# Attention probabilities in a hybrid decoder layer: transposes on fp32r operands fed by SBUF-to-SBUF transfers, and splits moved to the head of a unit

## The chip, the cores and the metric

The kernel runs on one core of a Trainium2 chip. The core has five engines that run side by side and are kept in step by semaphores: TensorE (matmuls and transposes), VectorE, ScalarE, GpSimd and SyncE. In the profile they are called PE, DVE, ACT, POOL and SP; PEld is TensorE's load of the stationary operand. Sixteen DMA engines move data between memories; a transfer is issued by one of the engines' queues (here SP's, and for a few transfers ACT's). The on-chip memory SBUF holds the operands, PSUM receives what TensorE produces.

The metric is the device time of one execution in microseconds. Before the change three runs took 390.55, 390.63 and 391.24 us, median 390.63.

## The reference

One layer of a causal decoder for 256 tokens of width 1024, all in float32. From a normalised input one wide projection gives queries, keys and values of two attention branches and the logits of two merge gates.

```
h = rmsnorm(x, g_mix);  proj = h @ w_in
o_a = nsa_attention(...)        # 8 heads, 2 key groups; compressed, selected and window branches, gated
o_b = dilated_attention(...)    # 12 heads in 3 groups, mixed by their softmax denominators
mixed = sigmoid(g_A) * (o_a @ w_proj_nsa) + sigmoid(g_B) * (o_b @ w_proj_dil)
x = x + mixed @ w_out
x = x + conv_ffn(rmsnorm(x, g_ffn))
return rmsnorm(x, g_final)
```

Each attention branch is softmax(q k - slope * distance) @ v under a causal mask. The product with v contracts over the keys, so the probabilities, which come out of the softmax with queries on the partitions and keys along the free axis, have to be transposed once.

## The kernel before

**Arithmetic.** Most products are made of three fp32r matmuls: each operand is split into a high part (rounded to fp32r) and a low part (the remainder, also fp32r), and high x high, high x low and low x high are summed in PSUM. fp32r is a four-byte type that TensorE takes in one pass; an engine that writes a tile of this type rounds. `split_hi` (line 127, ScalarE) and `split_lo` (line 131, VectorE, for a few units GpSimd) do this for the weights. Smaller products, among them probabilities times v, are plain fp32, which TensorE takes as two instructions each. A transpose is one TensorE instruction with the data as stationary operand and an identity as moving operand.

**Units.** The work is a list of units, mostly one block of 128 x 2048 weights (1 MB) each: 0 to 15 project queries, keys and values, 16 to 19 the logits of gate A, 20 to 23 those of gate B (`ev_ml`), 24 to 26 the projections of the two branches with the merge, 27 to 30 w_out, and the rest the ffn. The schedule is written out by hand in one loop over the units (lines 1127 to 1222). In each turn the host code emits, for every engine in this order, the load of the unit five ahead (SP), then some work of the attention, then the low part of the next unit's weights (`lo_of(i + 1)`), then the unit's matmuls, the high part for the unit after next (`hi_of(i + 2)`) and the evacuation of the unit's result, and then the attention's TensorE work. Each engine executes its own instructions in the order of emission. Loads wait for one of three raw weight buffers to come free, which the low part of an earlier unit does.

**Attention items.** Twelve items lie on units 9 to 20, one each: six of the NSA branch (class `Nsa`), six of the dilated one (class `Dil`), each with one or two heads and one half (t) of the queries; unit 11 also has the compressed branch (`Cmp`). An item at unit i goes through these steps:

- unit i: `split` (dilated items with t = 1 only) at the head, and `qk` after the matmuls: TensorE makes the scores in PSUM.
- unit i + 1: `sm` (VectorE adds the distances and takes the minimum, ScalarE the exponential, into a tile E, two buffers), and behind the weights' low part `sm2` (VectorE multiplies E by the gates and the inverse sums).
- unit i + 2: `tr`, behind the unit's matmuls: TensorE transposes E in blocks of 128 x 128 into PSUM (lines 881, 993 and 808); 8 blocks for an NSA item, 6 for a dilated one, 2 for the compressed branch.
- unit i + 3: `te` at the head: ScalarE, and for a part VectorE, copies the transposed blocks to SBUF (lines 886, 887, 998, 999, 813).
- units 14, 17, 20 and 23: `pv` for three items at a time (lines 894 and 1018), and in the unit after it `fin`, the split of the result.

**The split of a dilated item** (lines 935 to 939) copies one half of q and k as high parts to the other partitions (three ScalarE copies into a tile DK) and takes the low parts (two VectorE subtractions). `dil_tiles`, at unit 15, makes the tiles and zeroes a part of them on GpSimd. In the loop both stand behind `te` and `sm`:

```
for it in at(i - 3):  it.te()
for it in at(i - 1):  it.sm()
if i == FIRST_ITEM + 6:  dil_tiles()
for it in at(i):  if isinstance(it, Dil): it.split()
```

**Places in SBUF.** A tile's tag names its place. Tag MA (8 KB per partition) holds a part of the first weights and then gate A's logits; tag MB (8 KB) a part of the first weights, then the tile XC for the compression MLP until unit 8, and from unit 20 gate B's logits. Between units 8 and 20 MB is idle.

Of the kernel before, what the change touches and what calls it, by code (L numbers as in the profile page):

```python
# [11 lines left out]
F32 = mybir.dt.float32  # L12
# [6 lines left out]
S = 256  # L19
# [73 lines left out]
def build(ctx, tc, a, out):  # L93
# [143 lines left out]
    def bc(R, n):  # L237
# [16 lines left out]
    first = [att.tile([128, n * 768 + 8 * (t == "QS")], F32, name="first", tag=t)  # L254
             for n, t in zip(CHUNKS, ("QS", "MA", "qb", "MB", "kb", "vb"))]
    M = {}
# [56 lines left out]
    def ev_cmp(u):  # L313
        R = rt["R"]
        t = att.tile([128, 2, 2, 128], F32, name="E", tag="E", bufs=2)
        f = att.tile([128, 4, 256], F32, name="XC", tag="MB")
        p = u.p.rearrange("p i (s two) -> p two i s", two=2)
# [144 lines left out]
    ML = {}  # L462

    def ev_ml(i):
        def f(u):
            ab = i // 4
            if i % 4 == 0:
                ML[ab] = att.tile([128, 8, S], F32, name="ML%d" % ab, tag="MA" if ab == 0 else "MB")
            ev_k(ML[ab], 2 * (i % 4))(u)
        return f  # L470
# [7 lines left out]
    def mix_out(i, h, hook=None):  # L478

        if h == 0:  # L480
            mixh.append(att.tile([128, 4, S], F32R, name="mixh", tag="E", bufs=2))
            mixl.append(att.tile([128, 4, S], F32R, name="mixl", tag="PT", bufs=3))
        hs = slice(4 * i + 2 * h, 4 * i + 2 * h + 2)
        ho = slice(2 * h, 2 * h + 2)
        m = ML[0][:, hs]
        V.tensor_tensor(out=m, in0=m, in1=ML[1][:, hs], op=OP.add)
        A.activation(mixh[i][:, ho], m, AF.Copy)
        if hook:
            hook()
        V.tensor_sub(mixl[i][:, ho], m, mixh[i].bitcast(F32)[:, ho])  # L490

    def mm_pd(u):
        for h in range(4):
            p = mmT(u, [2 * h, 2 * h + 1], 2, OB['h'], OB['l'], "do"[h % 2])
            mB = ML[1][:, 2 * h:2 * h + 2]
            V.tensor_tensor(out=mB, in0=p, in1=mB, op=OP.mult)
            if h % 2:
                mix_out(0, h // 2)

    def mm_pn(i):  # L500
        def f(u):
            for h in range(2):
                p = mmT(u, [2 * h, 2 * h + 1], 4, oah, oal)
                m = ML[0][:, 4 * i + 2 * h:4 * i + 2 * h + 2]
                V.tensor_tensor(out=m, in0=p, in1=m, op=OP.mult)
                if i:
                    mix_out(1, h, None if h else between)
        return f
# [256 lines left out]

    class Cmp:
        def by_keys(self):
            p = cmp_["cm"][:, 256:512]
# [36 lines left out]
        def tr(self):  # L805
            p = pd([S], "o")
            for t in range(2):
                T.transpose(p[:, t * 128:(t + 1) * 128], self.E[:, t].rearrange("p h c -> p (h c)"), ident)
            self.pt = p

# [13 lines left out]

    class Nsa:

# [16 lines left out]
        def sm(self):  # L843
            js, t, nk, n = self.js, self.t, self.nk, self.n
            E = att.tile([128, 1024], F32, name="E", tag="E", bufs=2)
            self.E = E[:, :n * nk].rearrange("p (a k) -> p a k", a=n)
            st_ = att.tile([128, 24], F32, name="ast", tag="ast", bufs=2)
# [26 lines left out]
        def tr(self):  # L874
            self.sl = [(c, k, b, g) for c in range(len(self.js)) for k in range(self.nk // 128)
                       for b in range(2) for g in range(2)]
            self.pt = []
            for q in range(2):
                p = pd([4, 128], "t")
                for i, (c, k, b, g) in enumerate(self.sl[4 * q:4 * q + 4]):  # L880
                    T.transpose(p[:, i], self.E[:, 4 * c + 2 * g + b, k * 128:(k + 1) * 128], ident)  # L881
                self.pt.append(p)

# [38 lines left out]

    class Dil:

# [43 lines left out]
        def sm(self):  # L968
            ss, t, nk = self.ss, self.t, self.nk
            E = att.tile([128, 1024], F32, name="E", tag="E", bufs=2)  # L970
            self.E = E[:, :3 * len(ss) * nk].rearrange("p (c g k) -> p c g k", c=len(ss), g=3)
            st_ = att.tile([128, 24], F32, name="ast", tag="ast", bufs=2)
# [14 lines left out]
        def tr(self):  # L987
            self.sl = [(c, k, q) for k in range(self.nk // 128) for q in range(3) for c in range(len(self.ss))]
            self.pt = []
            for i in range(0, 6, 4):  # L990
                p = pd([4, 128], "t")
                for n, (c, k, q) in enumerate(self.sl[i:i + 4]):
                    T.transpose(p[:, n], self.E[:, c, q, k * 128:(k + 1) * 128], ident)
                self.pt.append(p)

# [84 lines left out]
    k = 0  # L1080
# [35 lines left out]
    def at(i):  # L1116
        return items.get(i, [])
# [9 lines left out]
    for i, u in enumerate(units):  # L1127
        load_to(i + LA)
        if i == 9:
            cmp_sum()  # L1130
        for it in batches.get(i - 1, []):
            it.fin()
        for it in at(i - 3):
            it.te()
        if i == 11:
            cmp_kv_ev()
        for it in at(i - 1):
            it.sm()
        if i == FIRST_ITEM + 6:
            dil_tiles()  # L1140
        for it in at(i):
            if isinstance(it, Dil):
                it.split()
        if i > 2 and i != 6:
# [17 lines left out]
        if i in (23, 24):  # L1162
            m = ML[i - 23]
            A.activation(m, m, AF.Sigmoid)
        if i == NFIRST:
# [121 lines left out]
```

## Time and profile before

| what | value |
|---|---|
| median of three runs | 390.63 us |
| the profiled execution | 391.16 us |
| its span | 389.3 us |
| TensorE granted clock, mean | 0.997 |
| TensorE, VectorE, ScalarE, GpSimd busy | 382.1, 300.0, 216.9, 31.3 us |
| moved by DMA | 72.62 MB, mean 187 GB/s |
| transposes of NSA, dilated, compressed items | 48, 36, 2 |
| units 9 to 23 on TensorE (start to end) | 47.4 to 164.1 us |

The span is the time between the first and the last recorded instruction; what is left of the execution's time lies outside it. Busy time of TensorE is counted from modelled ends of pipelined instructions, and overlapping instructions count once, so its share says little about how densely it works; the distance between the starts of successive instructions says more. Unit boundaries are found in the chain of waits by the groups of 32 and 16 matmuls of a unit (lines 186 and 191). A time in the chain's rows is the start in the span, followed by the length; in rows of one line's instructions the three durations are the minimum, median and maximum in nanoseconds.

### The profile page before, as it was taken

What the parts mean: (1) busy time and instruction counts of PE and PEld (TensorE: products, weight loads), DVE (VectorE), ACT (ScalarE), POOL (GpSimd) and SP (SyncE); (2) the same over time, 40 slices, a digit from 0 to 9 for tenths busy, and PEclk for the clock granted to TensorE, in tenths of its full rate; (3) what the DMA queues carried; (4) which work ended last, traced back from release to release, by engine and by line L of the source; (5) the groups of instructions that cost most, each with busy time, mean ns of one, the idle gap of its engine ahead of it and who ended that gap; (6) DMA issues with size and microseconds to landing.
All of it is one profiled execution on the core that took longest, in us unless ns stands there. A gap on an engine that the chain in (4) does not pass through costs nothing.

```text
span 389.3 us, 8064 instructions
## 1 busy us (share of the span) xinstructions
PE 382.1 (98%) x3420; PEld 375.7 (97%) x3420; DVE 300.0 (77%) x510; ACT 216.9 (56%) x306; POOL 31.3 (8%) x60
## 2 busy tenths in 40 slices
PE   8999999999999999999999999999999999999993
PEld 7999999999999999999999999999999999999993
DVE  6797599994877776558887789778696886968764
ACT  6876536775974665754634666626365363643613
POOL 8100000001000000250333000000000000000001
PEclk9999999999999999999999999999999999999998
DMA  8999253445234345452547266574644646446202
GB/s 292 404 354 382 110 215 119 166 148 221 108 109 128 132 159 184 159 184 111 189 170 280 104 223 216 204 231 178 241 173 153 229 168 253 162 163 224 103 0 109
DMA packets 11844, 72.62 MB, mean 187 GB/s; under 512 B 1312, under 2 KB 1696, under 8 KB 4128
## 3 DMA queue, kind: packets, MB, share of 16 engines
q1 hardware_dynamic: 11376, 71.25, 50.1%
q10 hardware_dynamic: 432, 0.85, 0.6%
q8 instruction: 27, 0.44, 0.5%
q14 instruction: 9, 0.07, 0.0%
HBM read 71.05 MB, written 1.05 MB: 185 GB/s over the span
## 4 chain that ended last, share of the span: by engine, by line
PE 94%; DVE 2%; ACT 2%; issue 0%; POOL 0%; POOLq 0%; ACTq 0%
PE ps_d L186 26%; PE ps_d L191 13%; PE ps_o L186 13%; PE ps_s L617 8%; PE ps_t L617 7%; PE ps_o L191 6%; PE ps_d L343 3%; PE ps_d L290 3%; PE ps_t L186 2%; PE ps_o L894 1%; PE ps_o L533 1%; PE ps_t L881 1%; PE ps_s L186 1%; PE ps_o L1018 1%; PE ps_t L191 1%; PE ps_t L1064 1%
## 5 line engine op out<-in xcount | busy, mean ns | idle before, releaser
L131 DVE TENSOR_TENSOR wlo<-raw,whi 128x2048 fp32r<-128x2048 f32 (+2 forms) x62 | 134.6, 2176 | 2.8 <-ACT whi L127 2.4
L127 ACT ACTIVATE whi<-raw 128x2048 fp32r<-128x2048 f32 (+2 forms) x62 | 115.1, 1858 | 32.7 <-DMA raw<-in_wts_dram 28.8
L186 PE MATMUL ps_d<-hTh,whi 128*128 128x256 f32 x384 | 90.4, 281 | 0.0
L186 PE MATMUL ps_d<-hTl,whi 128*128 128x256 f32 x384 | 89.3, 278 | 0.0
L186 PEld LDWEIGHTS ps_d<-hTh,whi 128*128 128x128 f32 x384 | 72.3, 188 | 0.9 <-issue 0.7
L186 PEld LDWEIGHTS ps_d<-hTl,whi 128*128 128x128 f32 x384 | 72.3, 188 | 0.0
L191 PE MATMUL ps_d<-hTh,wlo 128*128 128x256 f32 x384 | 47.9, 277 | 0.0
L191 PEld LDWEIGHTS ps_d<-hTh,wlo 128*128 128x128 f32 x384 | 45.8, 188 | 0.0
L186 PE MATMUL ps_o<-hTh,whi 128*128 128x256 f32 x160 | 36.9, 277 | 0.0
L186 PE MATMUL ps_o<-hTl,whi 128*128 128x256 f32 x160 | 36.8, 276 | 0.0
L572 ACT ACTIVATE C<-U,small 128x256 f32<-128x256 f32 x22 | 12.0, 594 | 43.7 <-DVE U L568 43.7
L186 PEld LDWEIGHTS ps_o<-hTl,whi 128*128 128x128 f32 x160 | 30.0, 188 | 0.0
L186 PEld LDWEIGHTS ps_o<-hTh,whi 128*128 128x128 f32 x160 | 30.0, 188 | 0.0
L576 DVE SCALAR_TENSOR_TENSOR C<-U,small,C 128x256 f32<-128x256 f32 x44 | 19.4, 482 | 7.5 <-ACT C L572 7.4
L858 ACT ACTIVATE E<-E,ast 128x256 f32<-128x256 f32 (+1 forms) x32 | 14.2, 451 | 10.1 <-DVE ast L853 10.1
L191 PE MATMUL ps_o<-hTh,wlo 128*128 128x256 f32 x160 | 19.8, 276 | 0.0
L191 PEld LDWEIGHTS ps_o<-hTh,wlo 128*128 128x128 f32 x160 | 18.9, 188 | 0.0
L568 DVE TENSOR_TENSOR U<-ps_d,R 128x512 f32<-128x512 f32 x6 | 4.1, 690 | 13.7 <-PE ps_d L191 10.7
L1123 DVE STREAM_TRANSPOSE X<-xT 32x256 f32<-32x256 f32 x32 | 13.9, 436 | 0.4
L1243 POOL TENSOR_TENSOR tiny<-cst,tiny 128x1 f32<-128x1 f32 x2 | 0.4, 192 | 166.7 <-ACT sq L1242 166.7
L131 POOL TENSOR_TENSOR wlo<-raw,whi 128x1024 fp32r<-128x1024 f32 x3 | 7.7, 2571 | 74.0 <-ACT whi L127 74.0
L617 PE MATMUL ps_s<-whi,al 128*128 128x256 f32 x88 | 12.1, 276 | 0.0
(272 smaller groups left out, 743.1 us busy)
## 6 DMA issues: line engine op xcount, KB each, us to landing
raw<-in_wts_dram SPq DMA_DIRECT2D x59, 1024.0 KB, 4.8
first<-in_first_dram SPq DMA_DIRECT2D x7, 384.0 KB, 6.0
raw<-in_wts_dram SPq DMA_DIRECT2D x2, 560.0 KB, 9.5
xn<-in_xn_dram SPq DMA_DIRECT2D x2, 512.0 KB, 9.5
w1k<-in_wts_dram SPq DMA_DIRECT2D x2, 512.0 KB, 7.0
w1v<-in_wts_dram SPq DMA_DIRECT2D x2, 512.0 KB, 7.9
xT<-in_xT_dram SPq DMA_DIRECT2D x1, 1024.0 KB, 7.0
gf<-in_g_final_dram ACTq DMA_DIRECT2D x1, 512.0 KB, 3.6
```

Of the source, the lines that this page charges most:

```text
L127: A.activation(u.hi[:, u.o + c0:u.o + c1], u.raw[:, c0:c1], AF.Copy)
L131: (eng or V).tensor_sub(u.lo[:, u.o + c0:u.o + c1], u.raw[:, c0:c1], u.hi.bitcast(F32)[:, u.o + c0:u.o + c1])
L186: T.matmul(po, l, r, start=start and bank not in banks, stop=False, skip_group_check=True)
L191: T.matmul(po, l, r, start=False, stop=stop and n == len(ks) - 1, skip_group_check=True)
L290: T.matmul(u.p[:, i], l[:, kt, i * 128:i * 128 + 128], r[:, kt], start=kt == 0 and i == 0 and q == 0, stop=kt == 7 and q == 2, skip_group_ ...
L343: T.matmul(u.p[:, i], l[:, kt, i * 128:i * 128 + 128], r[:, kt], start=kt == 0 and i == 0 and q == 0, stop=kt == 7 and q == 2, skip_group_ ...
L568: V.tensor_tensor(out=U[:, :, 2:], in0=u.p, in1=bc(rt["R2"], 2), op=OP.mult)
L572: A.activation(C[:, c], U[:, c, 2:], AF.Identity, scale=CW(2, t), bias=CB[:, t:t + 1])
L576: V.scalar_tensor_tensor(C[:, c], U[:, c, w:w + S], CW(w, t), C[:, c], op0=OP.mult, op1=OP.add)
L617: T.matmul(ffn["y"][t][ch][:, b:e] if own is None else own, x[:, kt, t * 128:t * 128 + 128], w[:, kt, ch * 512 + b:ch * 512 + e], start=st ...
L858: A.activation(self.E[:, i], self.E[:, i], AF.Exp, bias=mn[:, i:i + 1], scale=-1.0, accum_out=dn[:, i:i + 1])
L1123: V.transpose(X[32 * j:32 * j + 32, t].rearrange("p (k c) -> p k c", c=128)[:, :, 32 * b:32 * b + 32], xT[32 * b:32 * b + 32, :, t * 128 + ...
```

## The change

All 86 transposes of probabilities take fp32r operands. For this E, which is an fp32 tile, is moved word by word into a second tile Er of type fp32r by a DMA from SBUF to SBUF on ScalarE's queue (`send`), so that nothing is rounded. A copy of the identity in fp32r is made by ScalarE at unit 9. `send` of the item at unit i - 2 is emitted at the head of unit i, ahead of everything of that unit but the load; it waits for that item's `sm2`, which ran in unit i - 1, and `tr` at the end of unit i reads Er. The PSUM tile of a transpose has type fp32r too and is read as fp32 by `te`. The order of the blocks and their number stay.

Er lies in the idle place of gate B: tag MB is cut into MB0 and MB1 of 4 KB per partition, which the items take in turn (the compressed piece, and all items sent from unit 20 on, take MB1). Gate B's logits become two tiles of half the size (ML1 in MB0 from unit 20, in MB1 from unit 22), gate A's stay one tile seen in two halves. The two sigmoids of 2048 columns become four of 1024.

In the loop `dil_tiles` and `split` move ahead of `te` and `sm`; they come behind `send` and `fin`.

```diff
-             for n, t in zip(CHUNKS, ("QS", "MA", "qb", "MB", "kb", "vb"))]
+             for n, t in zip(CHUNKS, ("QS", "MA", "qb", "MB0", "kb", "vb"))]
...
-        f = att.tile([128, 4, 256], F32, name="XC", tag="MB")
+        f = att.tile([128, 4, 256], F32, name="XC", tag="MB0")
...
-            ab = i // 4
-            if i % 4 == 0:
-                ML[ab] = att.tile([128, 8, S], F32, name="ML%d" % ab, tag="MA" if ab == 0 else "MB")
-            ev_k(ML[ab], 2 * (i % 4))(u)
+            ab, c = i // 4, 2 * (i % 4)
+            if c % 4 == 0:
+                if ab == 0 and c == 0:
+                    m = att.tile([128, 8, S], F32, name="ML0", tag="MA")
+                    ML[0, 0], ML[0, 1] = m[:, :4], m[:, 4:]
+                elif ab:
+                    ML[1, c // 4] = att.tile([128, 4, S], F32, name="ML1", tag="MB%d" % (c // 4))
+            ev_k(ML[ab, c // 4], c % 4)(u)
...
     class Cmp:
+        def send(self, tag):
+            self.Er = att.tile([128, 256], F32R, name="Er", tag=tag)
+            nc.scalar.dma_start(self.Er.bitcast(F32), self.E.rearrange("p t h c -> p (t h c)"))
...
-            p = pd([S], "o")
+            p = ps.tile([128, S], F32R, name="ps_o", tag="o", bufs=2)
             for t in range(2):
-                T.transpose(p[:, t * 128:(t + 1) * 128], self.E[:, t].rearrange("p h c -> p (h c)"), ident)
-            self.pt = p
+                T.transpose(p[:, t * 128:(t + 1) * 128], self.Er[:, t * 128:(t + 1) * 128], rt["identr"])
+            self.pt = p.bitcast(F32)
...
+    class Item:
+        def send(self, tag):
+            r = att.tile([128, 1024], F32R, name="Er", tag=tag)
+            n = self.Ef.shape[1]
+            nc.scalar.dma_start(r[:, :n].bitcast(F32), self.Ef)
+            self.Er = r
+        def turned(self, blocks):
+            p = ps.tile([128, len(blocks), 128], F32R, name="ps_t", tag="t", bufs=2)
+            for n, b in enumerate(blocks):
+                T.transpose(p[:, n], self.Er[:, b * 128:b * 128 + 128], rt["identr"])
+            return p.bitcast(F32)
...
         load_to(i + LA)
+        if i == FIRST_ITEM:
+            rt["identr"] = att.tile([128, 128], F32R, name="identr")
+            A.activation(rt["identr"], ident, AF.Copy)
+        for it in at(i - 2):
+            it.send("MB%d" % (isinstance(it, Cmp) or i > 19 or i % 2 == 0))
         if i == 9:
             cmp_sum()
         for it in batches.get(i - 1, []):
             it.fin()
+        if i == FIRST_ITEM + 6:
+            dil_tiles()
+        for it in at(i):
+            if isinstance(it, Dil):
+                it.split()
         for it in at(i - 3):
             it.te()
         if i == 11:
             cmp_kv_ev()
         for it in at(i - 1):
             it.sm()
-        if i == FIRST_ITEM + 6:
-            dil_tiles()
-        for it in at(i):
-            if isinstance(it, Dil):
-                it.split()
...
         if i in (23, 24):
-            m = ML[i - 23]
-            A.activation(m, m, AF.Sigmoid)
+            for c in range(2):
+                m = ML[i - 23, c]
+                A.activation(m, m, AF.Sigmoid)
```

The `tr` methods of `Nsa` and `Dil` call `turned` twice, for the blocks in the same order as before.

More of the change, by code (lines that the diff above doesn't have):

```diff
@@ L462, in build, with ml @@
     ML = {}
+    def ml(ab, c):
+        return ML[ab, c // 4][:, c % 4:c % 4 + 2]
     def ev_ml(i):
         def f(u):
-            ab = i // 4
-            if i % 4 == 0:
-                ML[ab] = att.tile([128, 8, S], F32, name="ML%d" % ab, tag="MA" if ab == 0 else "MB")
-            ev_k(ML[ab], 2 * (i % 4))(u)
+            ab, c = i // 4, 2 * (i % 4)
[6 more added lines that the diff above has]
+            ev_k(ML[ab, c // 4], c % 4)(u)
         return f
@@ L482, in mix_out @@
             mixl.append(att.tile([128, 4, S], F32R, name="mixl", tag="PT", bufs=3))
-        hs = slice(4 * i + 2 * h, 4 * i + 2 * h + 2)
         ho = slice(2 * h, 2 * h + 2)
-        m = ML[0][:, hs]
-        V.tensor_tensor(out=m, in0=m, in1=ML[1][:, hs], op=OP.add)
+        m = ml(0, 4 * i + 2 * h)
+        V.tensor_tensor(out=m, in0=m, in1=ml(1, 4 * i + 2 * h), op=OP.add)
         A.activation(mixh[i][:, ho], m, AF.Copy)
@@ L494, in mm_pd @@
             p = mmT(u, [2 * h, 2 * h + 1], 2, OB['h'], OB['l'], "do"[h % 2])
-            mB = ML[1][:, 2 * h:2 * h + 2]
+            mB = ml(1, 2 * h)
             V.tensor_tensor(out=mB, in0=p, in1=mB, op=OP.mult)
@@ L503, in f @@
                 p = mmT(u, [2 * h, 2 * h + 1], 4, oah, oal)
-                m = ML[0][:, 4 * i + 2 * h:4 * i + 2 * h + 2]
+                m = ml(0, 4 * i + 2 * h)
                 V.tensor_tensor(out=m, in0=p, in1=m, op=OP.mult)
@@ L823, in build @@
     oA, oB = {}, {}
-    class Nsa:
+    class Item:
[9 more added lines that the diff above has]
+            return p.bitcast(F32)
+    class Nsa(Item):
         def __init__(self, js, t):
@@ L845, in sm @@
             E = att.tile([128, 1024], F32, name="E", tag="E", bufs=2)
-            self.E = E[:, :n * nk].rearrange("p (a k) -> p a k", a=n)
+            self.Ef = E[:, :n * nk]
+            self.E = self.Ef.rearrange("p (a k) -> p a k", a=n)
             st_ = att.tile([128, 24], F32, name="ast", tag="ast", bufs=2)
@@ L876, in tr @@
                        for b in range(2) for g in range(2)]
[L877 to L882, printed above, removed]
+            kb = self.nk // 128
+            self.pt = [self.turned([(4 * c + 2 * g + b) * kb + k for c, k, b, g in self.sl[q:q + 4]]) for q in (0, 4)]
         def te(self):
@@ L921, in dil_tiles @@
             P.memset(kl.bitcast(F32)[64 - up * 64:128 - up * 64], 0.0)
-    class Dil:
+    class Dil(Item):
         def __init__(self, ss, t):
@@ L970, in sm @@
             E = att.tile([128, 1024], F32, name="E", tag="E", bufs=2)
-            self.E = E[:, :3 * len(ss) * nk].rearrange("p (c g k) -> p c g k", c=len(ss), g=3)
+            self.Ef = E[:, :3 * len(ss) * nk]
+            self.E = self.Ef.rearrange("p (c g k) -> p c g k", c=len(ss), g=3)
             st_ = att.tile([128, 24], F32, name="ast", tag="ast", bufs=2)
@@ L988, in tr @@
             self.sl = [(c, k, q) for k in range(self.nk // 128) for q in range(3) for c in range(len(self.ss))]
[L989 to L994, printed above, removed]
+            kb = self.nk // 128
+            self.pt = [self.turned([(3 * c + q) * kb + k for c, k, q in self.sl[i:i + 4]]) for i in (0, 4)]
         def te(self):
```

## The prediction

> **What bounds the kernel now.** I read the page first (busy shares and the chain of waits), then stretches of the span cut at the attention units, then the chain in order of time, then the instructions of single lines.
>
> ```profile
> span 389.3 us, 8064 instructions
> PE 382.1 (98%) x3420; PEld 375.7 (97%) x3420; DVE 300.0 (77%) x510; ACT 216.9 (56%) x306; POOL 31.3 (8%) x60
> PE 94%; DVE 2%; ACT 2%; issue 0%; POOL 0%; POOLq 0%; ACTq 0%
> ```
>
> ```profile
> 45.50:54.30 8.80, 8.80 (x122) 8.46 (x122) 8.52 (x13) 2.19 (x2) 0.00 (x0) 1.00 0.25 91
> 69.60:76.90 7.30, 7.30 (x63) 7.08 (x62) 7.16 (x33) 6.10 (x21) 0.00 (x0) 1.00 0.26 92
> 84.40:95.05 10.65, 10.65 (x117) 9.98 (x116) 5.91 (x19) 5.94 (x14) 1.47 (x2) 1.00 0.73 278
> 134.00:143.50 9.50, 9.40 (x99) 8.87 (x98) 7.51 (x13) 5.64 (x7) 0.00 (x0) 1.00 0.35 117
> 150.00:156.30 6.30, 6.30 (x56) 6.30 (x55) 3.26 (x4) 2.45 (x3) 0.00 (x0) 1.00 0.74 268
> 156.30:164.10 7.80, 7.80 (x86) 7.50 (x85) 3.54 (x4) 5.51 (x4) 2.12 (x1) 1.00 0.47 167
> 164.10:202.00 37.90, 37.90 (x336) 37.90 (x335) 30.03 (x33) 20.23 (x19) 11.44 (x8) 1.00 0.46 167
> ```
>
> In the stretches the columns are length, then PE, PEld, DVE, ACT, POOL busy, granted clock, DMA share and GB/s. TensorE sets the end: it is filled in every stretch, and in the attention only 134.00 to 143.50 holds idle time. A matmul's recorded length is modelled and pipelined, so what counts is the pace, a group's length in the chain over its count. VectorE is the close second: 7.16 of 7.30 us at 69.60. A nanosecond off TensorE in the attention (units 9 to 23) is therefore a nanosecond off the end, unless VectorE, ScalarE or the new transfers then come too late.
>
> **The transposes.** The change touches 86: six NSA items of 8, six dilated items of 6, and 2 of the compressed branch.
>
> ```profile
> 90.78 0.87 PE ps_t L881 x8
> 91.65 2.77 PE ps_o L894 x48
> 116.03 0.66 PE ps_t L993 x6
> 141.45 2.12 PE ps_o L1018 x36
> 225.47 3.63 PE ps_d L186 x32
> ```
>
> ```profile
> L881 PEld LDWEIGHTS ps_t<-ident,E x48: 138/141/146, 68.3 to 109.3; 128*128 128x128 f32 x48
> L894 PEld LDWEIGHTS ps_o<-PT,Vn x96: 132/137/137, 91.6 to 119.1; 128*64 128x64 f32 x96
> L231 PEld LDWEIGHTS ps_o<-ident,tiny x8: 188/190/192, 18.9 to 214.1; 128*128 128x128 f32 x8
> L770 PE MATMUL ps_o<-qa,kc x8: 379/391/403, 67.7 to 68.0; 128*32 128x256 f32 x8
> L839 PE MATMUL ps_s<-KH,QS x16: 276/334/398, 52.9 to 90.3; 128*128 128x512 f32 x8, 128*128 128x256 f32 x8
> 210.46 0.52 PEld L218 LDWEIGHTS ps_o<-cst,acc 128*128 128x128 f32 x4
> ```
>
> A transpose costs 0.87/8 or 0.66/6 = 109 ns, 86 x 0.109 = 9.4 us in all. Two things could set that pace: the load of E, or the 128 columns of the identity streaming through. The rows speak for the stream. An fp32 matmul 256 wide (L770) lasts 391 ns, as long as an fp32r one 512 wide (L839, 398) and not as one 256 wide (276): fp32 streams at half the rate. From L839, 256 more fp32r columns cost 398 - 276 = 122 ns, so 128 at the half rate cost about 122 ns and at the full rate 61. And the load of a transpose is recorded with 141 ns, near the 64-column load of L894 (137) and far from the ordinary 128-column load (190). Where the load binds whatever is streamed, L218 with one column, the pace is (0.52 - 0.19)/3 = 110 ns; a load 49 ns shorter can't be what holds a transpose to 109.
>
> With fp32r operands the stream halves and the short load remains. No row shows such a transpose. The lower bound is the quickest row with a load of that length and 128 columns, L894: 2.77/48 = 58 ns; the upper is an ordinary fp32r pair, L186: 3.63/32 = 113 ns. I take L1018, 2.12/36 = 59 ns, since both the load's length and half the fp32 stream point there. That is 86 x (109 - 59) = **4.3 us** off TensorE, with the ends 86 x 51 = 4.4 off and 86 x 4 = 0.3 on.
>
> A rule speaks against this. The Trainium skill, "TensorE: Matmul & The Clock Gate", section "LDWEIGHTS (loading the stationary operand)", gives a load its columns over 1.2 GHz, 107 ns for 128, without regard to what streams. By it, as an estimate, the transposes stay at 107 to 109 ns and this term is nothing. The trace agrees with it for L218 (110 ns) and differs from it in the short loads of the transposes; so I keep it as a rival, below.
>
> **The transfers.** Thirteen moves SBUF to SBUF on ScalarE's queue: six of 512 KB, six of 384 KB, one of 128 KB, at the head of the unit that transposes them at its end. None like it is in the trace.
>
> ```profile
> gf<-in_g_final_dram ACTq DMA_DIRECT2D x1, 512.0 KB, 3.6
> out_dram<-Y SPq DMA_DIRECT2D x1, 512.0 KB, 2.6
> w1k<-in_wts_dram SPq DMA_DIRECT2D x2, 512.0 KB, 7.0
> L1169 ACTq DMA_DIRECT2D gf<-in_g_final_dram x1: 334/334/334, 207.2 to 207.2; - x1
> ```
>
> The bounds of a landing are 2.6 us (the store) and 7.0 us (the w1k load in the crowded start). I take gf's 3.6: same size and queue, weights flowing beside it. Issuing costs ScalarE 13 x 0.33 = 4.3 us, covered by its 44% idle time. What matters is landing before the transposes.
>
> ```profile
> 78.57 0.43 DVE L803 TENSOR_TENSOR Ec<-Ec,cst 128x256 f32<-128x256 f32 x1
> 83.70 1.14 DVE L872 TENSOR_SCALAR E<-E,ast 128x256 f32<-128x256 f32 x4
> 84.54 0.58 ACT L886 ACTIVATE PT<-ps_t 128x512 f32<-128x512 f32 x1
> 101.88 0.48 DVE L872 TENSOR_SCALAR E<-E,ast 128x128 f32<-128x128 f32 x2
> 108.79 0.87 PE ps_t L881 x8
> 149.42 0.65 PE ps_t L993 x6
> 155.73 0.66 PE ps_t L993 x6
> ```
>
> The tight ones: item 12 is normalised by 83.70 + 1.14 = 84.84 and transposed at 90.78. VectorE is busy without a break there and does not get earlier, TensorE does, by three NSA items and the compressed pair, 26 x 0.05 = 1.3 us: it wants E at 89.5, the transfer lands at 88.4. Item 20 goes to MB1 as item 19 did, so its transfer waits for the transposes that end at 149.42 + 0.65 = 150.07; from there to 155.73 are 5.7 us, against 3.6. Item 14, ready at 101.88 + 0.48 and transposed at 108.79, has 6.4 less 0.4 that its unit gains, 6.0 us; read in the same way items 11 and 15 lie between 5.5 and 6, the rest have more. The compressed piece (128 KB) is ready at 79.00 and wanted at about 82.8. No stall, cost nothing; past a landing of 4.7 us item 12 begins to pay.
>
> What queues behind a waiting send on ScalarE: the evacuation of the item before (te) and the exponentials. In unit 13 the send of the compressed branch waits for L803, to 79.0, and holds te by 1.5 us; TensorE asks for those PSUM buffers only at 83 less 0.8. In unit 14 te (84.54) moves to about 85. Its cover is the 5.6 us of matmuls before the next transposes. The E buffer is now freed by the transfer and not by the transposes, which takes away this VectorE wait of 0.71 us; it is off TensorE's path:
>
> ```profile
> 69.45 0.29 DVE L853 CUSTOM_DVE_ANT_0 E<-ps_s,tab 128x128 f32<-128x128 f32 x1 [0.71 <-PE ps_t L881]
> ```
>
> **The splits at the head.** Four dilated items, each with three ScalarE copies (0.52 + 0.83 + 0.84 us) and two VectorE subtractions (0.55 + 0.95), now ahead of te, of the softmax and of the low part of the next weights.
>
> ```profile
> 138.21 0.55 DVE L938 TENSOR_TENSOR DK<-qb,DK 64x384 fp32r<-64x384 f32 x1 [1.71 <-ACT DK L935]
> 137.65 0.52 ACT L935 ACTIVATE DK<-qb 64x384 fp32r<-64x384 f32 x1
> 138.08 0.83 ACT L936 ACTIVATE DK<-kb 64x768 fp32r<-64x768 f32 x1
> 138.93 0.85 ACT DK L937
> 139.83 0.97 PE ps_s L958 x6
> DVE DK L938 <- ACT DK L935: 6.2, 4, 1.7
> 139.83 0.42 PEld L958 LDWEIGHTS ps_s<-DK 128*128 128x128 f32 x3 [0.29 <-ACT DK L937]
> ```
>
> VectorE waited 6.2 us in four places for the copy of q, because ScalarE did the exponentials first. Once it cost TensorE: 0.29 us at 139.83. At the head the copies run during the first third of the unit, some 4 us before L958 asks; TensorE's gain of 0.3 us per unit is less than the 1.7 us that VectorE gets back. Gain **0.3 us**. What pays is te and the exponentials, 2.2 us later on ScalarE; their next user is again at the unit's end. The copies may now wait for L958 of the unit before (it reads the same q), which ends before the head. The zeroing on POOL at unit 15 moves ahead of one softmax; POOL is idle there. SP's loads wait for the low parts, which come earlier or as before.
>
> **The rest, at nothing.** One copy of the identity on ScalarE (2.19 busy of 8.80 us at 45.50). The sigmoid in four pieces for two adds about 0.2 us each to ScalarE (5.51 of 7.80 at 156.30). ML1's second half waits for the last transposes, 0.4 us for VectorE (3.26 of 6.30 at 150.00). After 164.10 TensorE has no gaps, and loads follow freed buffers, so what is gained passes to the end.
>
> **Sum.** -4.3 - 0.3 = -4.6 us. The profiled execution took 391.16 us, 1.9 of it outside the span, and becomes 386.6; it lies 0.5 above the median of the runs, so 390.63 - 4.6 = **386.0**.
>
> **Rivals.**
> *The load holds.* An fp32r transpose is bound by its 128-column load or by load and stream in series, at 109 to 113 ns. For it: L218 and L186 at 110 and 113 with any stream. Against it: the 141 ns loads. Time: 390.6 - 0.3 + (0 to 0.3) = 390.3 to 390.6. This is where the skill's rule on loads leads. The same time results if fp32 and fp32r transposes are one and the same to the array, so that the change only moves data.
> *The transfers land late.* At w1k's 7.0 us, the unit-end transposes wait by what lies past their room above: item 11 1.4 us, item 12 1.0 more (the stall before it widens its room), 14 and 15 1.0 to 1.4 each, 20 1.3: some 6 us against 4.6, so 392.0, slower. It decides from a landing of about 6.5 us. For it: w1k, and 278 GB/s at 84.40; against it: 92 GB/s at 69.60 and 117 at 134.00, and gf.
> *Two passes.* A short fp32r stream takes double time, or the array takes fp32r transposes as ordinary products in two steps: 86 x 109 = 9.4 more, 399.7. Against it: L839 at 256 columns is one pass. No fp32r matmul of 128 columns is in the trace to exclude it.
>
> **Chances.** Forecast 0.64 (its own range 385.4 to 387.5, a stall or two of item 12 or 20 included); the load holds 0.20; late transfers 0.10, of which a third leaves a gain; two passes 0.06. A change under 0.2% (0.8 us) can't be told from none here. Faster 0.64 + 0.03 = 0.67; same 0.20 less a little for late transfers beside it, 0.18; slower 0.15. The range 385.2 to 391.3 holds the forecast and the first rival, and leaves the two slow ones out.
>
> **What would show it.** Right: eight transposes at about 0.47 us and six at 0.35 in the chain; VectorE's wait for L935 down from 6.2 to under 3; L958 without a wait; thirteen transfers on ScalarE's queue landing in 3 to 4.5 us; no TensorE wait for a transfer at L-lines of the transposes. Wrong: groups of 0.87 again (the load), of 1.7 (two passes), or gaps ahead of the transposes in units 14 and 22 (late landings).

## The result and the profile after

The changed kernel took **395.56 us** (median of ten executions, 387.76 to 396.42) beside 390.60 for the kernel before (ten executions, 390.20 to 391.24): 1.3% slower, where 386.0 and a range up to 391.3 were forecast. The ten fall into two groups with nothing between them: four of 387.76 to 389.79 and six of 395.45 to 396.42. Comparisons below use executions of the quicker group alone, and over these four (median 388.6) the ratio is 0.9949 with an interval of [0.9932, 0.9967]. What divides the groups turned out to be the main finding. The profiled execution, 396.12 us, is one of the long ones.

The page of the changed kernel: its span, the busy shares, the chain by engine and the new transfers.

```profile
span 394.3 us, 8102 instructions
PE 387.3 (98%) x3420; PEld 381.6 (97%) x3420; DVE 300.0 (76%) x510; ACT 216.5 (55%) x309; POOL 30.9 (8%) x60
PE 97%; issue 0%; ACT 0%; POOL 0%; DVE 0%; POOLq 0%; ACTq 0%
Er<-E ACTq DMA_DIRECT2D x6, 512.0 KB, 4.6
Er<-E ACTq DMA_DIRECT2D x6, 384.0 KB, 5.5
```

TensorE is still what sets the end, and it is busy 5 us longer, though it was given less to do. The transfers take 1.0 and 1.9 us longer to land than the 3.6 us that were forecast. Where the time went shows in the chain in order of time (start, length, what), in which each group's length over its count is taken as its pace. After:

```profile
75.99 0.65 PE ps_t L848 x8
...
124.68 0.47 PE ps_t L848 x6
...
178.19 5.55 PE ps_o L539 x48
183.74 3.77 PE ps_o L186 x32
...
224.32 3.77 PE ps_d L186 x32
...
382.61 2.84 PE ps_s L623 x24
```

And the same stretch of the kernel before, with a group from its start:

```profile
34.20 3.77 PE ps_d L186 x32
...
180.80 5.45 PE ps_o L533 x48
186.25 3.63 PE ps_o L186 x32
...
377.79 2.73 PE ps_s L617 x24
```

Two things are to be read here. First, eight transposes now take 0.65 us and six 0.47, which is some 79 ns each: less than the 109 of before, more than the 59 forecast. Through the attention the change gains about what this gives, 86 x 30 ns: the first w_out unit starts at 178.19 instead of 180.80, 2.6 us earlier. Secondly, from there on all is lost again. The first w_out unit takes 5.55 us instead of 5.45, and behind it 32 matmuls take 3.77 us instead of 3.63, that is 118 ns each instead of 113, up to the last group (118 against 114). From the start of w_out to the end of the matmuls it is 385.45 - 178.19 = 207.3 us against 380.52 - 180.80 = 199.7. The sum -2.6 + 7.5 and 0.1 at the tail is the +5.0 of the two profiled executions (391.16 to 396.12). The granted clock is 1.00 in both from w_out to the last matmul (mean over the span 0.995 against 0.997), so it isn't the clock. Nor is 118 ns new: the kernel before had it at 34.20.

So three questions: why the pace changes in a part of the kernel that the change did not touch, why a transpose takes 79 ns, and what the late transfers cost.

### The profile page after: what moved, and what is told of

It is laid out like the page before. It is cut to its first block, busy times and chain, and to the rows that moved or that the text cites. A ratio compares the mean times of both kernels' runs of the same rounds, so it can differ in the third digit from the quotient of the medians.

```text
span 394.3 us, 8102 instructions
## 1 busy us (share of the span) xinstructions
PE 387.3 (98%) x3420; PEld 381.6 (97%) x3420; DVE 300.0 (76%) x510; ACT 216.5 (55%) x309; POOL 30.9 (8%) x60
## 4 chain that ended last, share of the span: by engine, by line
PE 97%; issue 0%; ACT 0%; POOL 0%; DVE 0%; POOLq 0%; ACTq 0%
PE ps_d L186 28%; PE ps_d L191 14%; PE ps_o L186 13%; PE ps_s L623 8%; PE ps_t L623 7%; PE ps_o L191 6%; PE ps_d L343 3%; PE ps_d L290 3%; PE ps_t L186 2%; PE ps_t L848 2%; PE ps_o L539 1%; PE ps_o L917 1%; PE ps_s L186 1%; PE ps_o L1038 1%; PE ps_t L191 1%; PE ps_t L1084 1%
## 5 line engine op out<-in xcount | busy, mean ns | idle before, releaser
L186 PE MATMUL ps_d<-hTh,whi 128*128 128x256 f32 x384 | 91.5, 282 | 0.0
L186 PE MATMUL ps_d<-hTl,whi 128*128 128x256 f32 x384 | 90.4, 279 | 0.0
L186 PE MATMUL ps_o<-hTh,whi 128*128 128x256 f32 x160 | 38.2, 282 | 0.0
L186 PE MATMUL ps_o<-hTl,whi 128*128 128x256 f32 x160 | 38.1, 281 | 0.0
L574 DVE TENSOR_TENSOR U<-ps_o,R 128x512 f32<-128x512 f32 x5 | 3.5, 690 | 12.4 <-PE ps_o L191 12.4
```

The costliest lines, as they stand in the source:

```text
L186: T.matmul(po, l, r, start=start and bank not in banks, stop=False, skip_group_check=True)
```

## The experiments

### 1. The pace behind w_out: is it the wait in the first unit?

The first w_out unit (`mm_out(0)`) takes its operand in the order in which the merge makes it ready: three parts of the contraction, each high x high, then `wh` with `mixl`, then `wl` with `mixh`. In its last part TensorE's load of `mixl` comes right behind its making. The instructions in order of time, VectorE's and TensorE's, before:

```profile
184.32 0.69 DVE L490 TENSOR_TENSOR mixl<-ML,mixh 128x512 fp32r<-128x512 f32 x1 [0.70 <-ACT mixh L487]
185.06 0.54 PEld L533 LDWEIGHTS ps_o<-mixl,whi 128*128 128x128 f32 x4
```

and after:

```profile
181.78 0.69 DVE L496 TENSOR_TENSOR mixl<-ML,mixh 128x512 fp32r<-128x512 f32 x1 [0.70 <-ACT mixh L493]
182.53 0.54 PEld L539 LDWEIGHTS ps_o<-mixl,whi 128*128 128x128 f32 x4
```

Counted from the start of the unit, the load of before comes at 185.06 - 180.80 = 4.26 us and `mixl` is ready at 4.21: 0.05 us behind. After, `mixl` is ready at 182.47 - 178.19 = 4.28, and the load comes at 4.34, 0.06 behind. So the 0.05 of before was no slack: there these loads come in their regular place, 0.45 us behind the four ahead of them, just as `mixl` allows it; after, they come 0.53 behind. My theory: this wait of about 0.1 us throws the stream of loads and matmuls behind it into the slower of two paces. The rival: something the change did to memory or to queues (the new places, the transfers) lowers the pace, and the wait is a by-product.

Two edits use `mixl` last in that part, in the changed kernel, which takes the wait away, and in the kernel before as a control; two more delay the merge in the kernel before; and the changed kernel ran once more as it is.

```diff
 # a2_mixl_last (on the changed kernel) and b2_mixl_last (on the kernel before)
-                for q, (l, r) in enumerate(((wh, mixh), (wh, mixl), (wl, mixh))):
+                for q, (l, r) in enumerate(((wh, mixh), (wl, mixh), (wh, mixl)) if k0 == 6
+                                           else ((wh, mixh), (wh, mixl), (wl, mixh))):
 # b1_late (on the kernel before; b3_late3 with three such memsets)
+        if i and h:
+            V.memset(tiny[:, 13:14], 0.0)
         V.tensor_tensor(out=m, in0=m, in1=ML[1][:, hs], op=OP.add)
```

> The changed kernel once more. Both theories: executions at about 388 to 389 us and at about 396 us. Theory W (a wait): in a slow execution the groups of 32 matmuls of the ffn last 3.77 us from a gap of some 0.07 us ahead of the third part of the first w_out unit on, in a fast one 3.63 us and there is no such gap. Rival E (the environment: granted clock, or traffic that the change left behind): the pace changes at some other place, or without a gap.

> The changed kernel with one edit: in the last part of the first w_out unit the products that need the low part of the mixture come after those that need the high part, 0.45 us later. Theory W: the gap is gone in every execution, all of them at 387.5 to 389.5 us, none at 395 or more; ratio to before 0.994. Rival E: slow executions as often as without the edit, about 6 in 10, at 396 us.

> The kernel before with one small VectorE instruction (a memset of one column, about 0.06 to 0.1 us) ahead of the last sum of the merge, so that the low part of the mixture comes later by that. Theory W: TensorE now waits some 0.05 us at the third part of the first w_out unit and the pace after it becomes 117.8 ns: all or most executions at about 397 us, 7 us over before. Rival E: 390.6 to 390.7 us.

> The kernel before with the same reordering as a2_mixl_last. Theory W and rival E: 390.6 us, no difference, since before never waited there (its load of the weights comes 0.05 us after the low part is ready).

> The kernel before with three small VectorE instructions ahead of the last sum of the merge (the one of b1_late moved nothing, it fell into a pause of VectorE); together they make the low part of the mixture about 0.2 us later than before, so that TensorE must wait 0.1 us or more at the third part of the first w_out unit. Theory W: the pace behind the wait is a matter of chance, so that some of the executions, between 2 and 8 in 10, take 397 to 398 us and the others 390.7. Rival E (the slow executions have nothing to do with the wait): all at 390.6 to 390.8 us.

Measured: a1_again 388.31 us, so one of the quick group. a2_mixl_last 388.11 (387.51 to 389.21, six executions, none long), ratio 0.9929 [0.9906, 0.9953]. b1_late 390.56, 0.9988 [0.9970, 1.0007]. b2_mixl_last 390.57, 0.9994 [0.9979, 1.0009]. b3_late3: nine executions of 390.35 to 391.80, and three of 397.92, 398.09 and 400.09; over the nine the ratio is 1.0011 [1.0000, 1.0021]. The chain at w_out of a1_again, of a2_mixl_last and of b3_late3, each in a quick execution:

```profile
177.92 5.55 PE ps_o L539 x48
183.47 3.63 PE ps_o L186 x32
```

```profile
178.46 5.44 PE ps_o L539 x48
183.90 3.63 PE ps_o L186 x32
```

```profile
180.56 5.60 PE ps_o L536 x48
186.16 3.63 PE ps_o L186 x32
```

What follows. With the order changed the wait is gone (5.44), and so are the long executions. The changed order alone is worth nothing (b2_mixl_last). b1_late decides nothing: its memset fell into a pause of VectorE, `mixl` came no later. With three memsets the kernel before, which has neither the transfers nor the new places, has the wait (5.60) and has long executions 7 to 9 us above the others. The kernel before itself, run beside all these, stays at or below 392.88 us in 84 executions. And a1_again corrects the theory in one point: the wait is there (5.55) and the pace stays at 3.63. The wait doesn't set the slow pace; it makes it possible, and which of the two follows differs from execution to execution.

The same is seen a second time in the 14 profiles, at their head, in units that no edit touches. In the changed kernel TensorE's load at 19.46 waits for a high part:

```profile
19.46 0.19 PEld L186 LDWEIGHTS ps_s<-whi,hTh 128*128 128x128 f32 x1 [0.20 <-ACT whi L127]
```

It starts 0.39 us behind the load ahead of it, in the profile of the kernel before 0.30, and in the other twelve 0.11. In those two the units behind it, up to 45 us, go at 118 ns (3.77 at 34.20 above), in the other twelve at 113. At neither place does a profile show the slow pace without such a delay ahead of it.

### 2. Where the late `mixl` comes from

The delay is small enough to be followed instruction by instruction: ScalarE's sigmoid of gate B, GpSimd's second low part for the next weights, VectorE's low part beside it, the first sum of the last merge. The kernel before:

```profile
164.49 1.91 ACT L1164 ACTIVATE ML<-ML 128x2048 f32<-128x2048 f32 x1
...
171.10 2.94 POOL L131 TENSOR_TENSOR wlo<-raw,whi 128x1024 fp32r<-128x1024 f32 x1 [0.41 <-ACT whi L127]
...
170.56 1.22 DVE L131 TENSOR_TENSOR wlo<-raw,whi 128x1024 fp32r<-128x1024 f32 x1
...
173.28 1.30 DVE L486 TENSOR_TENSOR ML<-ML,ML 128x512 f32<-128x512 f32 x1
...
177.16 0.68 DVE L486 TENSOR_TENSOR ML<-ML,ML 128x512 f32<-128x512 f32 x1
```

The changed kernel:

```profile
161.88 2.00 ACT L1190 ACTIVATE ML<-ML 128x1024 f32<-128x1024 f32 x2
...
168.49 3.02 POOL L131 TENSOR_TENSOR wlo<-raw,whi 128x1024 fp32r<-128x1024 f32 x1 [0.31 <-ACT whi L127]
...
167.96 1.30 DVE L131 TENSOR_TENSOR wlo<-raw,whi 128x1024 fp32r<-128x1024 f32 x1
...
170.68 1.38 DVE L492 TENSOR_TENSOR ML<-ML,ML 128x512 f32<-128x512 f32 x1
```

The sigmoid in two pieces takes 2.00 us instead of 1.91. ScalarE's next high part starts that much later, and with it the piece of the low part that GpSimd makes ahead of the one shown: before, it runs from 168.28 to 170.69 and reaches 0.13 us into VectorE's piece (1.22); after, from 165.76 to 168.17, it reaches 0.21 us into it. From there 0.08 us is handed on: VectorE's low part lasts 1.30 instead of 1.22, GpSimd's 3.02 instead of 2.94, and the merge's sum 1.38 instead of 1.30. That sum takes 0.68 us by itself (177.16); beside GpSimd it ends 0.54 us after GpSimd does before (174.58 against 174.04), and 0.55 after (172.06 against 171.51): the two engines take turns. The Trainium skill, "SBUF — State Buffer", section "Who interferes with whom", says that VectorE and GpSimd share a pair of ports, that this contention is an exclusive lock, and that a VectorE instruction with two SBUF inputs contends with a GpSimd instruction that reads SBUF; these rows agree. If this chain is the cause, the split of the sigmoid alone brings long executions to the kernel before:

```diff
 # b4_sigmoid2 (on the kernel before)
-            A.activation(m, m, AF.Sigmoid)
+            for c in range(2):
+                A.activation(m[:, 4 * c:4 * c + 4], m[:, 4 * c:4 * c + 4], AF.Sigmoid)
```

> The kernel before with one edit: each sigmoid of a gate in two pieces of 1024 columns for one of 2048, as the change has it. Theory W with its chain: 0.09 us more on ScalarE, GpSimd's part of the next low weights 0.09 us later, VectorE's last low part (1.22 us) and first sum of the merge (1.30) become 1.30 and 1.38 where they share with GpSimd, the low part of the mixture 0.08 us late, the first w_out unit's 48 products 5.55 us for 5.45, and by chance 2 to 8 executions in 10 at 397 to 398 us, the others at 390.7. Rival (the wait comes from the rest of the change: transfers, or TensorE being early): all at 390.5 to 390.8 us, 5.45 us.

Measured: six executions of 390.19 to 391.14 and six of 397.84 to 398.64. The quick six stand at 1.0002 [0.9991, 1.0012] to the kernel before. Its profiled execution is a long one (398.22 us):

```profile
163.99 2.00 ACT L1165 ACTIVATE ML<-ML 128x1024 f32<-128x1024 f32 x2
...
170.60 3.02 POOL L131 TENSOR_TENSOR wlo<-raw,whi 128x1024 fp32r<-128x1024 f32 x1 [0.32 <-DMA raw<-in_wts_dram]
...
172.78 1.38 DVE L486 TENSOR_TENSOR ML<-ML,ML 128x512 f32<-128x512 f32 x1
```

```profile
180.30 5.55 PE ps_o L533 x48
185.85 3.77 PE ps_o L186 x32
```

What follows. Splitting each of ScalarE's two sigmoids in two, and nothing else, gives the whole chain with the changed kernel's durations (2.00, 3.02, 1.38, 5.55, 3.77) and long executions some 7.4 us above the others, in half the cases. So this part of the change is enough to cause the loss, without its transposes or transfers. (The changed kernel with whole sigmoids was not run.) In the quick half the same edit costs nothing, as the prediction had it.

### 3. Why a transpose takes 79 ns

The prediction let the stream of the identity set the pace. To part the load of the stationary operand from the stream, e_pace makes each transpose of an item three times into the same place: with 96 of its 128 stationary columns, with 64 partitions (so that 64 columns stream and 128 stationary columns are loaded), and at last whole.

```diff
 # e_pace (on a2_mixl_last), in turned, ahead of the loop that is there
+            for n, b in enumerate(blocks):
+                T.transpose(p[:96, n], self.Er[:, b * 128:b * 128 + 96], rt["identr"])
+            for n, b in enumerate(blocks):
+                T.transpose(p[:, n, :64], self.Er[:64, b * 128:b * 128 + 128], rt["identr"][:64, :64])
```

> a2_mixl_last with three times the transposes, for their pace alone: each group is made once with 96 columns of the stationary operand, once on 64 partitions with an identity of 64 columns, and once whole (the last is what is used, so the result is whole). A whole fp32r transpose takes 79 ns. If the load of the stationary operand sets it: about 60 to 65 ns with 96 columns of it, and 79 with the short stream. If the stream of the identity sets it: 79 with 96 columns, and 45 or less with a stream of 64. If a fixed cost of load and stream in series sets it: both shorter, about 65 to 70.

TensorE's loads in order of time, four of each kind (start, length of the group), and the mean of one, in ns, behind the bar:

```profile
69.50 0.33 PEld L848 LDWEIGHTS ps_t<-identr,Er 128*96 128x96 f32 x4
69.90 0.39 PEld L850 LDWEIGHTS ps_t<-identr,Er 64*128 64x128 f32 x4
70.33 0.40 PEld L852 LDWEIGHTS ps_t<-identr,Er 128*128 128x128 f32 x4
```

```profile
L848 PEld LDWEIGHTS ps_t<-identr,Er 128*96 128x96 f32 x84 | 7.5, 125 | 1.2 <-issue 0.9
L850 PEld LDWEIGHTS ps_t<-identr,Er 64*128 64x128 f32 x84 | 8.3, 136 | 1.7
L852 PEld LDWEIGHTS ps_t<-identr,Er 128*128 128x128 f32 x84 | 8.4, 140 | 1.0
```

The distance of the starts is the group's length less one load, over three: 0.205 / 3 = 68 ns with 96 columns, 0.254 / 3 = 85 ns with half the stream, 0.26 / 3 = 87 ns whole. Over all groups the starts of the loads lie 70, 84 and 84 ns apart in the median. Halving the stream changes nothing; a quarter fewer stationary columns takes a sixth to a fifth off. The loads of the changed kernel's transposes lie 86 ns apart in the median; the 79 is lower because it counts matmuls, of which the second and third of all groups but the first start 57 to 67 ns behind the one ahead, and the rest 79 to 92. The whole execution took 407.37 us, with three times the transposes.

What follows. The pace of an fp32r transpose goes by the columns of its load. The 59 ns of L1018 and the 58 of L894 in the kernel before are no third point for this: their instructions start in pairs, 6 or 7 ns apart, and 109 to 110 ns pass from pair to pair, so that no row of that trace shows one load and one stream in 59 ns. The Trainium skill, "TensorE: Matmul & The Clock Gate", section "Back-to-back issue gap", gives 81 ns as the sustained spacing in a stream of loads and matmuls at N = 128 (streamed columns), set by both; 79 agrees, and as an estimate 86 x (109 - 81) = 2.4 us would have come from it. By the rule of the Trainium skill that the prediction weighed, 107 ns for any load of 128 columns, nothing would have been gained; the trace differs from it.

### 4. What the transfers cost, and what hides them

Three kernels take the change apart: the splits at the head alone; the fp32r transposes with their transfers alone; and the transfers alone, with transposes in fp32 as before. All three have the reordered part of w_out, so that no wait there disturbs them.

```diff
 # c1_splits (on b2_mixl_last): ahead of te and sm, and taken away behind them;
 # c2_fp32r (on a2_mixl_last): the reverse
+        if i == FIRST_ITEM + 6:
+            dil_tiles()
+        for it in at(i):
+            if isinstance(it, Dil):
+                it.split()
 # c3_moves (on c2_fp32r): Er, the PSUM tiles and the identity are fp32
-            r = att.tile([128, 1024], F32R, name="Er", tag=tag)
+            r = att.tile([128, 1024], F32, name="Er", tag=tag)
...
-                T.transpose(p[:, n], self.Er[:, b * 128:b * 128 + 128], rt["identr"])
-            return p.bitcast(F32)
+                T.transpose(p[:, n], self.Er[:, b * 128:b * 128 + 128], ident)
+            return p
```

> The kernel before, with the reordering of b2_mixl_last (390.57 us) and the splits of the dilated items moved to the head, nothing else of the change. As predicted: 0.3 us less, 390.3 us, VectorE's wait for the copy of q about 2.4 us for 6.2. If the splits cost something by holding the evacuation of the transposes back: 390.6 or more.

> The changed kernel with the reordering of a2_mixl_last (388.1 us), but with the splits back in their old place. If the gain is the transposes' alone: 86 x 0.03 us = 2.6 us less than 390.57, 388.0 us, as a2. If the splits carry a part of it (the stall at L958, or VectorE's lateness beside a faster TensorE): 388.4 us or more, up to 389 where the stall grows as TensorE gets ahead.

> As c2_fp32r, but Er, the identity and the PSUM tiles are of type fp32, so that the transfers are made and the transposes stay as they were. If the transfers are free: 390.6 us and groups of eight transposes at 0.87 us. If they cost by landing late or by slowing TensorE's reads: 391 us or more, with waits of TensorE for Er.

Measured beside 390.47 for the kernel before: c1_splits 390.17, ratio 0.9989 [0.9979, 0.9998]; c2_fp32r 390.92 (389.78 to 394.36), 1.0013 [0.9992, 1.0034]; c3_moves 392.66 (391.16 to 396.45), 1.0056 [1.0026, 1.0085]. The waits of TensorE (who waited for whom: us in all, times, longest) in c2_fp32r, and the one of c3_moves with two landings from its chain:

```profile
PE ps_t L848 <- DMA Er<-E: 1.6, 2, 1.0
PE ps_s L981 <- ACT DK L960: 0.8, 2, 0.6
```

```profile
PE ps_t L848 <- DMA Er<-E: 3.8, 2, 2.8
```

```profile
109.96 8.35 DMA Er<-E
...
137.38 6.93 DMA Er<-E
```

What follows. The parts don't add. Alone the transfers cost 2.2 us, the splits gain 0.3, and the fp32r transposes with their transfers give nothing (0.4 over, within the interval), since their 2.6 us go into 2.4 us of waits (388.0 to 389 was expected of c2_fp32r). With the splits at the head the whole (a2_mixl_last) is at 388.11. So the move of the splits is worth 2.9 us there (c2_fp32r is 0.4 over its 390.47, a2_mixl_last 2.5 under its 390.61): put first, they let ScalarE and VectorE finish the softmax, and with it the transfer, earlier. The transfer of item 15 starts 7.02 us behind the one ahead of it in a2_mixl_last (108.96 and 101.94), and 8.23 us in c2_fp32r (109.38 and 101.15). c3_moves scatters, and in its profiled execution (394.62 us) 3.8 us are these waits, while behind w_out it goes at the quicker pace:

```profile
189.68 3.63 PE ps_o L186 x32
```

In a2_mixl_last TensorE has one such wait left:

```profile
PE ps_t L848 <- DMA Er<-E: 0.3, 1, 0.3
```

It is for the transfer that starts at 108.96. VectorE's instructions of that kernel ahead of it, in order of time:

```profile
105.59 2.28 DVE L131 TENSOR_TENSOR wlo<-raw,whi 128x2048 fp32r<-128x2048 f32 x1
...
108.18 0.75 DVE L1009 TENSOR_SCALAR E<-E,ast 128x384 f32<-128x384 f32 x2
```

SP's queue of the same kernel there:

```profile
107.94 0.33 SPq L161 DMA_DIRECT2D raw<-in_wts_dram  x1
```

And ScalarE's:

```profile
108.96 0.47 ACTq L841 DMA_DIRECT2D Er<-E  x1
```

VectorE's low part ends at 105.59 + 2.28 = 107.87 and frees a raw weight buffer, and SP issues the next load of 1 MB at 107.94. The normalisation of E, next on VectorE, ends at 108.93, and the transfer follows at 108.96, 1.0 us behind the load, and lands at 115.09, 0.8 us behind that load. The order is that of the loop (`lo_of`, then `sm2`): eleven of the twelve items' transfers start 0.9 to 2.2 us behind a load of 1 MB and land in 3.9 to 7.7 us. The first starts 3.8 us behind one and lands in 3.0. d1_sp_first turns it round: the twelve items' transfers go on SP's queue ahead of the unit's load. d2_rounded does without them: VectorE's normalisation writes Er itself, for all but item 20 and the compressed piece. The probabilities are then rounded to fp32r.

```diff
 # d1_sp_first (on a2_mixl_last)
-            nc.scalar.dma_start(r[:, :n].bitcast(F32), self.Ef)
+            nc.sync.dma_start(r[:, :n].bitcast(F32), self.Ef)
...
-        load_to(i + LA)
+        for it in at(i - 2):
+            if not isinstance(it, Cmp):
+                it.send("MB%d" % (i > 19 or i % 2 == 0))
+        load_to(i + (4 if 9 <= i <= 22 else LA))
 # d2_rounded (on a2_mixl_last), Nsa and Dil alike
-                V.tensor_scalar(self.E[:, i], self.E[:, i], f[:, i:i + 1], None, op0=OP.mult)
+                V.tensor_scalar(to[:, i], self.E[:, i], f[:, i:i + 1], None, op0=OP.mult)
```

> a2_mixl_last (388.1 us) with the twelve large transfers on SP's queue, each ahead of the weight load that the same stretch of VectorE's work releases (loads emitted one unit later in units 9 to 22); the 128 KB piece stays on ScalarE's queue. If the landings of 4 to 8 us come from the 1 MB weight loads beside them: 3.0 to 3.6 us for nearly all, no wait of TensorE for Er, and 387.5 to 388.0 us. If an SBUF-to-SBUF transfer is that slow by itself: landings stay at 5 us and more, and the time at 388.1 or, with the loads later, above.

> a2_mixl_last without eleven of the twelve large transfers: VectorE's last product of the softmax writes Er directly, as fp32r, so that the probabilities are rounded to fp32r (this changes the computation: they are not rounded in the reference). Item 20 and the compressed piece keep their transfers. If the transfers cost time (0.3 us of waits in a2, and more by what they slow): 387.3 to 387.8 us. If they are free but for that wait: 387.8 to 388.1.

Measured beside 390.55: d1_sp_first 388.14, 0.9933 [0.9920, 0.9945]; d2_rounded 388.93 (387.89 to 390.82), 0.9957 [0.9941, 0.9973]. Landing and waits of d1_sp_first (the twelve items and the compressed piece, min/median/max):

```profile
DMA to landing us min/median/max: 2.8/3.2/5.7
```

```profile
PE ps_o L818 <- DMA Er<-Ec: 0.4, 1, 0.4
```

What follows. Ahead of the load eight of the twelve items' transfers land in 2.8 to 3.3 us, the others in up to 5.3, and TensorE no longer waits for an item; behind it they took 5.4 us in the median (3.0 to 7.7 in a2_mixl_last). The small transfer of the compressed branch, left on ScalarE's queue, now starts 1.6 us behind a load, is the late one (5.7 us) and costs 0.4, so that the time is that of a2_mixl_last. d2_rounded took longer than the 388.1 us that were expected at most: nothing is gained without eleven transfers, but TensorE waits 0.8 us for the one of item 20, so that it doesn't bound what the others cost. What TensorE waits for transfers is nothing in the profiled execution of the changed kernel and 0.3 us in a2_mixl_last, and a2_mixl_last, 0.7% below the kernel before, is the best version found; d1_sp_first can't be told from it.

## Why the prediction was wrong

**"After 164.10 TensorE has no gaps, and loads follow freed buffers, so what is gained passes to the end."** This step failed, and it alone turned a gain into a loss. There was no gap in the trace of before, but also no slack: one load came as late as `mixl` just allowed, so that 0.08 us more made a wait of as much, and the pace of the 200 us behind it was taken as given. The edit that brought the 0.08 us had been seen and priced, "about 0.2 us each to ScalarE", at nothing: right as far as ScalarE goes (0.09), but its covers were named no further than the engine itself. The kernel before had both paces in its trace, 3.77 at 34.20 and 3.63 at 186.25, and I read only one of them. The other rows needed were in the trace as well: `mixl` ready at 185.01 and loaded at 185.06. That the median is a long execution is chance at six to four: among the quick ones it would be 388.6, inside the stated range, and the sum of the forecast would still have been wrong by what follows.

**The transposes.** The gain was mis-sized: 86 x (109 - 79) = 2.6 us against 4.3. The bounds (58 to 113 ns) held. The failure was to take L1018 and L894 as nearest because their loads are recorded with the same 132 to 137 ns, and to read their length over count as the pace of one instruction. They load 64 columns, and two of them start together, a pair every 109 to 110 ns; the pace goes by columns (e_pace), while the recorded length of a load hardly does. What holds the new transposes is the load after all. Whether the stream held the fp32 ones at 109, as the prediction argued, no run parted. The rival "the load holds" had the right resource and too high a price.

**The transfers.** Landing was mis-sized: 4.6 and 5.5 us in the median instead of 3.6. I said that it would begin to pay past 4.7, at item 12, and judged by the mean traffic of a stretch; what counts is the load that SP issues 0.9 to 2.2 us ahead of a transfer. It pays at items 15 and 18 (c2_fp32r, c3_moves), not at 12. Yet in the changed kernel TensorE waits for no transfer, and 0.3 us for item 15 in a2_mixl_last. "The transfers land late" is what c2_fp32r and c3_moves show, at 0.4 and 2.2 us over the kernel before; the splits kept it from the change itself.

**The splits at the head.** By themselves as predicted: 0.3 us, and the stall ahead of the matmuls of the scores is gone. VectorE's wait went as forecast, from 6.2 us to under 3:

```profile
DVE DK L961 <- ACT DK L958: 2.4, 4, 1.1
```

Not seen was that they pay for the transfers' lateness, 2.9 us in all and so 2.6 beyond their own 0.3.

**The sum.** With the measured terms, the last being the wait of a2_mixl_last, it is 390.6 - 2.6 - 0.3 + 0.3 = 388.0; a2_mixl_last gives 388.11, the quick executions of the changed kernel 387.76 to 389.79. The forecast's own range, 385.4 to 387.5, missed that too, by the transposes. That the identity copy, the waits for the new gate places and the issue of the transfers on ScalarE cost nothing was not tested one by one; nothing of the sum is left for them.

## What to carry to other kernels

A long stream of loads and matmuls without gaps is not safe because nothing waits in it: look for the operand that is ready only just in time at its head, since a wait of a tenth of a microsecond there cost 7 us here, in some executions and not in others. Where a median jumps, list the executions before averaging, and compare the paces of equal groups in the chain of a long and a quick one. And price a matmul by a row with the same type and number of stationary columns, by the starts of its instructions and not by a group's length where two start together, and a transfer by what is issued just ahead of it.

## What the runs showed of the hardware that was not expected

- Streams of fp32r loads and matmuls, 128 stationary columns and 256 streamed, run at one of two paces, 113 ns (32 in 3.63 us) or 118 ns (3.77), at the same clock (1.00), and behind w_out keep it for 200 us. In the attention, where other matmuls come between, it changes from unit to unit (16 in 1.81 us at 51.26, 1.89 at 58.21, 1.81 at 65.10 in the kernel before). A wait of about 0.1 us can change it: 6 of 10 executions of the changed kernel, 6 of 12 of b4_sigmoid2 and 3 of 12 of b3_late3 were long, and of a2_mixl_last, d1_sp_first and d2_rounded, which have two-piece sigmoids but no wait there, none of 19. Why the stream keeps a pace, and what decides which, stays open: the long executions of b3_late3 were not profiled, and no run here looks inside the array. c2_fp32r and c3_moves, with no wait there either, scatter more than the others (up to 394.36 and 396.45); in their profiled executions (391.34 and 394.62) w_out goes at 113 ns, and TensorE waits 2.4 and 3.8 us ahead of it; their other executions were not profiled.
- An fp32r transpose of 128 x 128 takes 79 ns where an fp32 one takes 109, and its pace goes by the stationary columns (68 to 70 ns with 96 of them, beside 84 to 87 with 128), not by the columns streamed.
- Two fp32 instructions with 64 stationary columns (L894, L1018) start 6 or 7 ns apart, and a pair takes 109 to 110 ns, as long as one fp32 transpose with 128.
- A transfer of 384 or 512 KB inside SBUF lands in about 3 us when it is issued ahead of a load of 1 MB (2.8 to 3.3 in eight of twelve cases of d1_sp_first), and in 3.9 to 7.7 when it is issued 0.9 to 2.2 us behind one (a2_mixl_last); the small one of 128 KB lands in 3.2 us 4.3 behind a load (a2_mixl_last), and in 5.7 us 1.6 behind one (d1_sp_first). The Trainium skill, "DMA: Bandwidth & Descriptors", section "Anatomy of one DMA — SWDGE (gpsimd) path", fits transfers that GpSimd issues by 2.0 us and the bytes over 436 GB/s, as an estimate 2.9 and 3.2 us for the two sizes: on SP's queue most landings ahead of the load agree (2.8 to 2.9 and 3.2 to 3.3), those behind it don't.
